# A hybrid decoder block: indexer operands loaded early, query-key passes over 128 rows, softmax divided after the values

## The chip, the cores and the metric

The kernel runs on one core of a Trainium2 chip. The metric is device time in microseconds (us) of one execution. Engines: PE is TensorE (PEld its weight loads), DVE is VectorE, ACT is ScalarE, POOL is GpSimd, SP is SyncE. Each issues its instructions in a fixed order. TensorE's clock has two levels here, 1.2 and 2.4 GHz; the profile gives the granted clock as a share of the higher one.

## The reference, cut to what matters

One layer on 512 tokens of width 1024, in float32. A projection of the normalized input is split into a sparse attention, a recurrence (RWKV-7), a short convolution and three gates; the three results are gated, merged and projected, and a feed-forward part follows. The change concerns the attention:

```python
def one_block(args):                       # 128 queries of each of 4 blocks
    sc = einsum('bqhd,bsd->bqsh', qi_b, ki) * IDX_DIM ** -0.5
    score = einsum('bqsh,bqh->bqs', relu(sc), wi_b)          # the indexer: 8 heads of 64
    score = where(s_idx <= t_b, score, NEG_INF)
    _, sel = top_k(score, n_keep)                            # n_keep = 128
    logits = einsum('bqhd,bqkhd->bqhk', q_b, k[sel]) * ATTN_HEAD_DIM ** -0.5
    bias = rel_bias[t5_bucket(pos_b - positions[sel])]       # a bias by distance
    p = softmax(where(valid, logits + bias, NEG_INF))
    o = einsum('bqhk,bqkhd->bqhd', p, v[sel])                # 8 heads of 64
```

## The kernel before, in words

Matmul operands of 32 bits are split into a high and a low part (`whi`, `wlo`, `h_hi`, `h_lo`); a projection is three passes for each of eight blocks of 128 rows (`mm_t`, L177 to L179, 512 columns; for the value columns `mm_n`, L188 to L190, 256 columns). Weights come by SP's queue into a ring of four raw tiles, ACT makes the high part (L163), POOL the low part (L165, later DVE). A scheduler orders the instructions of each engine when the program is built; the order of the source is the priority. Memory is a stack of pools from the left and one from the right; a tile in reused space waits for the tiles that lay there.

The stages that matter here, in order:

- **Mask stage.** `att_cols` projects indexer queries (slot 2), then `ki` and `wi` (L766, L767), then queries and keys with the steps of `bias_steps` between them: DVE compares positions with thresholds into `mk` tiles (L721, a ring of 18 in the pool `bi`), TensorE sums them into bias tiles, which go to memory as `bias_d`. Queries and keys go to memory as `z_att`, `z_ki`, `z_wi`, each as a high and a low part.
- **Value columns** (L773 to L783), written as `z_v`. Then `bi` closes.
- **Indexer** (L803 to L843). The pools `att` and `ix` open where `bi` was. POOL issues the loads of `qi` (eight) and `ki` (two), SP those of `wiT` and `vtok`. For query blocks 1 to 3 and eight heads, `two_pass` multiplies queries with keys: the first pass takes 128 rows (high and low part of the query, against the high part of the key twice), the second the 64 rows of the high query against the low key. ACT applies relu, DVE sums the heads into `sc` (L832, L834), then finds 128 maxima by sixteen rounds of MAX8 and MATCH_REPLACE8 (L839, L840).
- **Attention** (L855 to L897), four pairs of heads by four query blocks, 16 steps. POOL adds bias and selection (`bt`), `two_pass` (L800, L801) makes the logits, DVE adds `bt` and takes the maximum (L874) and negates it (L876), ACT takes the exponential and its sum (L878), DVE takes the reciprocal and scales the probabilities (L881), TensorE transposes them (L885), ACT copies them to `pT` (L889). After four blocks, 16 matmuls with the values as weights (64 columns of them) and `pT` moving (L894) give the output transposed.
- Beside these stages the gate and branch projections of `branch(1)` and `branch(2)` fill TensorE, and `ada_parts` runs on DVE (L215, L217): it takes blocks of `ada_w` from SP's queue into a ring of three and sums them into `acc`. `branch(0)` needs the attention's output.

`sd_bank` gives one of five PSUM banks, `mm_bank` one of three.

## Time and profile before

| | us |
|---|---|
| median of 3 runs | 1195.21 |
| lowest, highest | 1187.89, 1198.48 |
| the profiled execution | 1197.88 |
| its span, first to last instruction | 1196.2 |
| TensorE busy in it | 1093.3 |
| VectorE busy in it | 763.9 |
| mean granted clock | 0.95 |

A profile row of instructions names the line, the engine, the operation, out<-in, shapes and how many (x); then busy us and mean ns, and after the second bar the engine's idle time just before them with what ended it. A timeline row begins with the start in us and the duration in us; a matmul's duration overlaps the next one's, so the distance of starts is what it costs in a stream.

### The profile page before, as it was taken

The page shows a single profiled execution, that of the slowest core. Times are in us where ns is not written, and L with a number is a line of the kernel's source. Part 1 is how long each engine was busy: PE and PEld are TensorE (multiplying, and loading weights), DVE is VectorE, ACT ScalarE, POOL GpSimd, SP SyncE. Part 2 cuts the span into 40 slices and gives each one's busy share as a digit, 9 for nine tenths or more (in the row PEclk, how much of TensorE's full clock was granted, in tenths as well). Part 3 has the DMA queues.
Part 4 walks back from the last instruction along what each step waited for, and adds up shares of the span by engine and source line. Part 5 has one row for each costly group of instructions (what it writes and reads, how often), then busy time and mean ns, then how long its engine had stood idle before and what let it go on. Part 6 is the DMA issues. An engine that isn't in the chain of part 4 may idle for free.

```text
span 1196.2 us, 17528 instructions
## 1 busy us (share of the span) xinstructions
PE 1093.3 (91%) x6710; PEld 877.2 (73%) x6710; DVE 763.9 (64%) x1363; ACT 447.3 (37%) x765; POOL 363.7 (30%) x254
## 2 busy tenths in 40 slices
PE   4889899799999989998887999998899999999996
PEld 3667678577767875876655778877898888888885
DVE  5888777732587828798555454468866766762326
ACT  4243332132334322422333443446543444542213
POOL 3233233322222430565455210003443455200001
PEclk9899899899989975998899999999999999999998
DMA  9641123322336990279766343522233333462201
GB/s 324 183 107 42 39 75 91 88 61 60 115 98 193 302 247 9 76 208 233 211 186 152 91 132 101 176 84 89 75 85 106 87 90 106 141 229 92 97 5 71
DMA packets 191074, 148.26 MB, mean 124 GB/s; under 512 B 18148, under 2 KB 167038, under 8 KB 190990
## 3 DMA queue, kind: packets, MB, share of 16 engines
q1 hardware_dynamic: 162605, 122.57, 35.5%
q10 hardware_dynamic: 23056, 14.53, 4.1%
q0 software_dynamic: 5328, 10.03, 3.8%
q8 instruction: 53, 0.87, 0.3%
q14 instruction: 32, 0.25, 0.1%
HBM read 128.48 MB, written 18.63 MB: 123 GB/s over the span
## 4 chain that ended last, share of the span: by engine, by line
PE 59%; DVE 21%; issue 8%; DMA 7%; ACT 3%; POOL 2%; SPq 0%; ACTq 0%; DVEq 0%; POOLq 0%
PE mm L177 6%; PE mm L179 6%; PE mm L178 6%; DMA xraw<-in_ada_w 3%; PE sd L177 2%; PE sd L178 2%; PE sd L179 2%; PE sd L801 2%; PE sd L1250 2%; PE sd L1252 2%; PE sd L1251 2%; PE sd L1047 2%; DVE acc L217 2%; PE sd L1049 2%; PE sd L1048 2%
## 5 line engine op out<-in xcount | busy, mean ns | idle before, releaser
L165 POOL TENSOR_TENSOR wlo<-wraw,whi 128x1024 fp32r<-128x1024 f32 (+1 forms) x70 | 157.1, 2246 | 279.6 <-ACT whi L163 222.1
L178 PE MATMUL mm<-h_lo,whi 128*128 128x512 f32 (+2 forms) x496 | 203.3, 410 | 1.5 <-DVE h_lo L1076 1.5
L177 PE MATMUL mm<-h_hi,whi 128*128 128x512 f32 (+2 forms) x496 | 203.7, 412 | 0.7 <-DVE o_cv L702 0.7
L179 PE MATMUL mm<-h_hi,wlo 128*128 128x512 f32 (+2 forms) x496 | 203.4, 410 | 0.0
L163 ACT ACTIVATE whi<-wraw 128x1024 fp32r<-128x1024 f32 (+1 forms) x86 | 80.2, 935 | 221.2 <-PE mm L178 95.2
L178 PEld LDWEIGHTS mm<-h_lo,whi 128*128 128x128 f32 (+1 forms) x496 | 96.2, 194 | 24.5 <-issue 3.3
L177 PEld LDWEIGHTS mm<-h_hi,whi 128*128 128x128 f32 (+1 forms) x496 | 96.0, 194 | 23.0 <-issue 4.2
L179 PEld LDWEIGHTS mm<-h_hi,wlo 128*128 128x128 f32 (+1 forms) x496 | 96.3, 194 | 22.1 <-issue 2.4
L1017 DVE TENSOR_TENSOR wlo<-wraw,whi 128x1024 fp32r<-128x1024 f32 x46 | 64.5, 1403 | 58.9 <-ACT whi L1016 58.3
L1016 ACT ACTIVATE whi<-wraw 128x1024 fp32r<-128x1024 f32 x46 | 48.7, 1059 | 75.7 <-PE sd L1252 27.7
L217 DVE SCALAR_TENSOR_TENSOR acc<-xraw,ccol,acc 128x512 f32<-128x512 f32 x56 | 55.7, 994 | 26.1 <-DMA xraw<-in_ada_w 25.7
L1034 POOL TENSOR_TENSOR fS<-wraw 128x512 f32<-128x512 f32 x13 | 19.8, 1526 | 155.3 <-DMA wraw<-in_ffn_w_up 142.5
L1047 PE MATMUL sd<-mg_hi,shi 128*128 128x256 f32 x156 | 45.1, 289 | 7.8 <-DVE p L1190 7.8
L1017 DVE TENSOR_TENSOR slo<-wraw,shi 128x1024 fp32r<-128x1024 f32 x28 | 34.9, 1247 | 21.6 <-ACT shi L1016 21.5
L721 DVE TENSOR_SCALAR mk<-posq,thr 128x512 f16<-128x512 f32 (+3 forms) x128 | 44.7, 424 | 4.1 <-PE sd L727 4.1
L1293 POOL TENSOR_TENSOR f<-f 128x512 f32<-128x512 f32 x4 | 5.7, 1415 | 134.8 <-ACT wk L993 134.8
L177 PE MATMUL sd<-h_hi,whi 128*128 128x512 f32 x112 | 44.5, 397 | 0.0
L1048 PE MATMUL sd<-mg_lo,shi 128*128 128x256 f32 x156 | 44.4, 285 | 0.0
L1049 PE MATMUL sd<-mg_hi,slo 128*128 128x256 f32 x156 | 44.4, 285 | 0.0
L178 PE MATMUL sd<-h_lo,whi 128*128 128x512 f32 x112 | 44.3, 396 | 0.0
L179 PE MATMUL sd<-h_hi,wlo 128*128 128x512 f32 x112 | 44.2, 395 | 0.0
L177 PE MATMUL mm<-o,whi 128*128 128x512 f32 x96 | 39.9, 416 | 3.2 <-DVE modc L203 3.2
(521 smaller groups left out, 2780.7 us busy)
## 6 DMA issues: line engine op xcount, KB each, us to landing
wraw<-in_w_in SPq DMA_DIRECT2D x61, 512.0 KB, 4.3
xraw<-in_ada_w SPq DMA_DIRECT2D x96, 256.0 KB, 4.4
wraw<-in_ffn_w_up SPq DMA_DIRECT2D x44, 512.0 KB, 3.9
wraw<-in_ffn_w_down SPq DMA_DIRECT2D x22, 512.0 KB, 3.4
wraw<-in_w_branch SPq DMA_DIRECT2D x24, 256.0 KB, 3.8
bias_d<-stage ACTq DMA_DIRECT2D x10, 512.0 KB, 5.2
wraw<-in_w_o SPq DMA_DIRECT2D x8, 512.0 KB, 3.8
z_att<-wk ACTq DMA_DIRECT2D x12, 256.0 KB, 2.2
```

What stands on the lines that cost most here:

```text
L163: ACT.activation(hi, raw, AF.Copy)
L165: lo_engine[0].tensor_tensor(lo, raw, hi, op=ALU.subtract)
L177: PE.matmul(ps, hi[:, k, :], ahi[:, k0 + k, :], start=start and k == 0, stop=False)
L178: PE.matmul(ps, hi[:, k, :], alo[:, k0 + k, :], start=False, stop=False)
L179: PE.matmul(ps, lo[:, k, :], ahi[:, k0 + k, :], start=False, stop=stop and k == kt - 1)
L217: DVE.scalar_tensor_tensor(acc, raw, ck, acc, op0=ALU.mult, op1=ALU.add)
L721: DVE.tensor_scalar(m_[:, :n], posq[:, b * 128:], thr[:, b, gg:gg + 1], None, op0=ALU.is_ge)
L1016: ACT.activation(hi, src, AF.Copy)
L1017: DVE.tensor_tensor(lo, src, hi, op=ALU.subtract)
L1047: PE.matmul(ps, w[0][:, k], b[0][:, k], start=first and k == 0, stop=False, skip_group_check=True)
L1048: PE.matmul(ps, w[0][:, k], b[1][:, k], start=False, stop=False, skip_group_check=True)
L1049: PE.matmul(ps, w[1][:, k], b[0][:, k], start=False, stop=k == 3, skip_group_check=True)
```

## The change

The pools `att` and `ix` open ahead of `bi` and stay beside it; the ring of `mk` has 16 tiles. The loads of `qi`, `ki` and `wiT` are issued by POOL right after `z_ki` and `z_wi` are written, ahead of the query and key projections; `vtok` stays where it was. The second pass of `two_pass` takes 128 rows (both query parts against the low key, twice), in the indexer and in the attention; `kl` is loaded twice for that. In the attention, DVE takes the negated logit and its minimum, each head's exponential follows at once, the transposes take the exponentials undivided, the values are multiplied for each query block with `pT` as weights, and the division is one DVE multiplication of the 128x128 result (`o_tok`), which four transposes then turn.

```diff
+    att = right_pool("att")
+    ix = right_pool("ix")
     bi = right_pool("bi")
...
-                    m_ = T("mk", [128, 512], F16, tag="mk", bufs=18, pool=bi.pool)
+                    m_ = T("mk", [128, 512], F16, tag="mk", bufs=16, pool=bi.pool)
...
     ACT.dma_start(z_wi, t[64:72])
+    vtok = T("vtok", [128, 4, 512], pool=att.pool)
+    sel = {0: cmask}
+    for qb in range(1, 4):
+        sel[qb] = T("sc", [128, (qb + 1) * 128], tag="sc%d" % qb, pool=att.pool)
+    qi = T("qi", [128, 4, 2, 384], F32R, pool=ix.pool)
+    for i in range(4):
+        load_q(qi[:, i], z_att[2, i], 128, 384)
+    ki = T("ki", [128, 2, 512], F32R, pool=ix.pool)
+    for hh in range(2):
+        POOL.dma_start(ki[hh * 64:(hh + 1) * 64], z_ki)
+    wiT = T("wiT", [8, 512], pool=ix.pool)
+    POOL.dma_start(wiT, z_wi)
     att_cols(C_ATT, 0, HD ** -0.5)
     att_cols(C_ATT + MIX, 1, 1.0)
...
     def two_pass(ps, q, hh, q0, k_hi, k_lo, n):
-        r = slice(hh * 64, hh * 64 + 64)
         PE.matmul(ps[:, :n], q[:, hh, q0:q0 + 128], k_hi[:, :n], start=True, stop=False)
-        PE.matmul(ps[:, :n], q[r, hh, q0:q0 + 128], k_lo[r, :n], start=False, stop=True)
+        PE.matmul(ps[:, :n], q[:, hh, q0:q0 + 128], k_lo[:, :n], start=False, stop=True)
...
-        kh, kl = M("kh", [128, 2, 512], F32R), M("kl", [128, 512], F32R)
-        for hh in range(2):
-            POOL.dma_start(kh[hh * 64:(hh + 1) * 64], z_att[1, pr, :, 0, :].rearrange("(h r) t -> r h t", h=2))
-        POOL.dma_start(kl, z_att[1, pr, :, 1, :])
-        pT = M("pT", [128, 4, 640], bufs=1)
+        kh, kl = M("kh", [128, 2, 512], F32R), M("kl", [128, 2, 512], F32R)
+        for i, k in enumerate((kh, kl)):
+            for hh in range(2):
+                POOL.dma_start(k[hh * 64:(hh + 1) * 64], z_att[1, pr, :, i, :].rearrange("(h r) t -> r h t", h=2))
+        o_tok = M("o_tok", [128, 4, 128], bufs=1)
...
-                DVE.tensor_tensor_reduce(lg[hh][:, :n], ps[:, :n], bt[:, hh, :n], 1.0, -3.0e38, op0=ALU.add, op1=ALU.max,
+                DVE.tensor_tensor_reduce(lg[hh][:, :n], ps[:, :n], bt[:, hh, :n], -1.0, 3.0e38, op0=ALU.add, op1=ALU.min,
                                          accum_out=rs[:, 0, hh:hh + 1])
-            DVE.tensor_scalar(rs[:, 1], rs[:, 0], -1.0, None, op0=ALU.mult)
+                ACT.activation(lg[hh][:, :n], lg[hh][:, :n], AF.Exp, bias=rs[:, 0, hh:hh + 1], scale=-1.0,
+                               accum_out=rs[:, 1, hh:hh + 1])
+            DVE.reciprocal(rs[:, 2], rs[:, 1])
+            po = sd_bank()
             for hh in range(2):
-                ACT.activation(lg[hh][:, :n], lg[hh][:, :n], AF.Exp, bias=rs[:, 1, hh:hh + 1], accum_out=rs[:, 2, hh:hh + 1])
-            DVE.reciprocal(rs[:, 0], rs[:, 2])
-            for hh in range(2):
-                DVE.tensor_scalar(lg[hh][:, :n], lg[hh][:, :n], rs[:, 0, hh:hh + 1], None, op0=ALU.mult)
                 pt = sd_bank()
                 for b in range(qb + 1):
-                    j = (b, qb - b)[hh]
-                    PE.transpose(pt[:, j * 128:(j + 1) * 128], lg[hh][:, b * 128:(b + 1) * 128], ident)
...
+                    PE.transpose(pt[:, b * 128:(b + 1) * 128], lg[hh][:, b * 128:(b + 1) * 128], ident)
+                pT = M("pT", [128, 512])
+                ACT.activation(pT[:, :n], pt[:, :n], AF.Copy)
+                h = 2 * pr + hh
+                for b in range(qb + 1):
+                    PE.matmul(po[:, hh * 64:(hh + 1) * 64], pT[:, b * 128:(b + 1) * 128], vtok[:, b, h * 64:(h + 1) * 64],
+                              start=(b == 0), stop=(b == qb))
+            DVE.tensor_tensor(o_tok[:, qb].rearrange("p (h d) -> p h d", h=2), po[:, :128].rearrange("p (h d) -> p h d", h=2),
+                              rs[:, 2].unsqueeze(2).to_broadcast([128, 2, 64]), op=ALU.mult)
         po = sd_bank()
-        for b in range(4):
-            for hh in range(2):
...
+        for qb in range(4):
+            PE.transpose(po[:, qb * 128:(qb + 1) * 128], o_tok[:, qb], ident)
         ACT.activation(o_at[:, pr, :], po, AF.Copy)
```

## Rows read from the trace of the kernel before

**Rows 1.** The page's first part: busy us, share of the span, instructions of each engine.

```profile
PE 1093.3 (91%) x6710; PEld 877.2 (73%) x6710; DVE 763.9 (64%) x1363; ACT 447.3 (37%) x765; POOL 363.7 (30%) x254
```

**Rows 2.** Stretches: length, busy us (instructions) of each engine, granted clock, DMA share, GB/s.

```profile
421.40:438.70 17.30, 12.63 (x85) 12.38 (x84) 0.75 (x1) 4.15 (x5) 5.74 (x4) 0.80 1.12 261
442.00:476.00 34.00, 34.00 (x64) 17.52 (x63) 25.48 (x77) 9.46 (x18) 2.10 (x4) 0.50 0.18 54
476.00:510.00 34.00, 34.00 (x149) 27.01 (x149) 24.90 (x48) 12.71 (x20) 17.92 (x12) 1.00 0.31 86
510.00:557.00 47.00, 43.77 (x190) 35.47 (x189) 46.83 (x76) 13.87 (x22) 30.72 (x20) 0.93 0.75 212
557.00:703.00 146.00, 124.62 (x532) 87.81 (x531) 80.93 (x184) 53.20 (x128) 57.42 (x44) 0.94 0.63 157
703.00:760.00 57.00, 57.00 (x248) 46.16 (x247) 27.08 (x36) 21.23 (x31) 2.95 (x4) 1.00 0.47 130
```

**Rows 3.** TensorE's timeline, last value matmuls and first score passes: start, us, instruction.

```profile
438.36 0.28 PE L188 MATMUL mm<-whi,h_hi 128*128 128x256 f32 x1
438.48 0.28 PE L189 MATMUL mm<-wlo,h_hi 128*128 128x256 f32 x1
...
439.14 0.39 PE L800 MATMUL sd<-ki,qi 128*128 128x256 f32 x1
439.46 0.38 PE L801 MATMUL sd<-ki,qi 64*128 64x256 f32 x1
```

**Rows 4.** TensorE's timeline in the value columns, idle before in brackets.

```profile
424.05 0.38 PE L188 MATMUL mm<-whi,h_hi 128*128 128x256 f32 x1 [2.63 <-ACT whi L163]
426.48 0.58 PE L189 MATMUL mm<-wlo,h_hi 128*128 128x256 f32 x1 [2.04 <-POOL wlo L165]
426.86 0.41 PE L190 MATMUL mm<-whi,h_lo 128*128 128x256 f32 x1
```

**Rows 5.** POOL's timeline: a low part in the mask stage, and the `qi` loads.

```profile
357.56 3.95 POOL L165 TENSOR_TENSOR wlo<-wraw,whi 128x1024 fp32r<-128x1024 f32 x1 [11.84 <-ACT whi L163]
...
414.53 4.82 POOL L796 DMA_DIRECT2D qi<-z_att  x8
```

**Rows 6.** The DMA view of 408 to 440: totals, then an issue with KB each, us.

```profile
DMA packets 8249, 8.52 MB, mean 266 GB/s; under 512 B 522, under 2 KB 6410, under 8 KB 8246
...
qi<-z_att POOLq DMA_DIRECT2D x8, 192.0 KB, 10.2
```

**Rows 7.** The page's costliest groups: the mask comparisons.

```profile
L721 DVE TENSOR_SCALAR mk<-posq,thr 128x512 f16<-128x512 f32 (+3 forms) x128 | 44.7, 424 | 4.1 <-PE sd L727 4.1
```

**Rows 8.** TensorE's timeline in the attention: values, projections, transposes.

```profile
604.77 2.85 PE L894 MATMUL sd<-pT,vtok 128*64 128x512 f32 x16
...
609.15 0.40 PE L178 MATMUL mm<-o,whi 128*128 128x512 f32 x1
609.39 0.40 PE L179 MATMUL mm<-o,wlo 128*128 128x512 f32 x1
...
635.42 1.11 PE L885 MATMUL sd<-ident,lg 128*128 128x128 f32 x8 [2.57 <-DVE lg L881]
```

**Rows 9.** Groups by line, 400 to 710 us: the softmax of the attention.

```profile
L878 ACT ACTIVATE lg<-lg,rs 128x128 f32<-128x128 f32 (+3 forms) x32 | 17.8, 557 | 30.3 <-DVE rs L876 30.3
L881 DVE TENSOR_SCALAR lg<-lg,rs 128x128 f32<-128x128 f32 (+3 forms) x32 | 16.9, 569 | 0.5
L874 DVE CUSTOM_DVE_ANT_0 lg<-sd,bt 128x128 f32<-128x128 f32 (+3 forms) x32 | 15.4, 490 | 25.8 <-PE sd L801 25.3
...
L889 ACT ACTIVATE pT<-sd 128x128 f32<-128x128 f32 (+3 forms) x32 | 12.5, 436 | 32.5 <-PE sd L885 32.5
```

**Rows 10.** Who waited for whom, 408 to 703 us: us in total, times, longest.

```profile
PE sd L885 <- DVE lg L881: 16.7, 10, 3.7
...
DVE acc L217 <- DMA xraw<-in_ada_w: 25.7, 15, 5.1
...
DVE wi L822 <- PE sd L821: 16.1, 1, 16.1
```

**Rows 11.** TensorE's timeline in the recurrence: matmuls of 128x128 weights, 64 columns.

```profile
258.85 1.67 PE L625 MATMUL sd<-UV,HYL 128*128 128x64 f32 x14
```

More of the change, by code (lines that the diff above doesn't have):

```diff
@@ L763, in att_cols, with load_q @@
             split_out(z_att[slot, i], z_col(c0 + i * 128), scale)
+    def load_q(dst, z, t0, n):
+        row = 2 * 512
+        for hh in range(2):
+            src = bass.AP(tensor=z.tensor, offset=z.offset + hh * 512 + t0, ap=[[row, 64], [64 * row + (1 - 2 * hh) * 512, 2], [1, n]])
+            POOL.dma_start(dst[hh * 64:(hh + 1) * 64], src)
     att_cols(C_ATT + 3 * MIX, 2, HD ** -0.5)
@@ L786, in hybrid_block @@
     op_ = left_pool("op")
-    def load_q(dst, z, t0, n):
-        row = 2 * 512
-        for hh in range(2):
-            src = bass.AP(tensor=z.tensor, offset=z.offset + hh * 512 + t0, ap=[[row, 64], [64 * row + (1 - 2 * hh) * 512, 2], [1, n]])
-            POOL.dma_start(dst[hh * 64:(hh + 1) * 64], src)
     def two_pass(ps, q, hh, q0, k_hi, k_lo, n):
-        r = slice(hh * 64, hh * 64 + 64)
         PE.matmul(ps[:, :n], q[:, hh, q0:q0 + 128], k_hi[:, :n], start=True, stop=False)
-        PE.matmul(ps[:, :n], q[r, hh, q0:q0 + 128], k_lo[r, :n], start=False, stop=True)
-    att = right_pool("att")
-    vtok = T("vtok", [128, 4, 512], pool=att.pool)
-    sel = {0: cmask}
-    for qb in range(1, 4):
-        sel[qb] = T("sc", [128, (qb + 1) * 128], tag="sc%d" % qb, pool=att.pool)
-    ix = right_pool("ix")
-    qi = T("qi", [128, 4, 2, 384], F32R, pool=ix.pool)
-    for i in range(4):
-        load_q(qi[:, i], z_att[2, i], 128, 384)
-    ki = T("ki", [128, 2, 512], F32R, pool=ix.pool)
-    for hh in range(2):
-        POOL.dma_start(ki[hh * 64:(hh + 1) * 64], z_ki)
-    wiT = T("wiT", [8, 512], pool=ix.pool)
-    SP.dma_start(wiT, z_wi)
+        PE.matmul(ps[:, :n], q[:, hh, q0:q0 + 128], k_lo[:, :n], start=False, stop=True)
     SP.dma_start(vtok, z_v.rearrange("b p n -> p b n"))
@@ L890, in hybrid_block @@
-        po = sd_bank()
-        for b in range(4):
-            for hh in range(2):
-                h = 2 * pr + hh
-                PE.matmul(po[hh * 64:(hh + 1) * 64, b * 128:], vtok[:, b, h * 64:(h + 1) * 64],
-                          pT[:, b, (b + 1) * 128:] if hh == 0 else pT[:, 3 - b, :(4 - b) * 128],
-                          start=(b == 0), stop=(b == 3), skip_group_check=True)
+                    PE.transpose(pt[:, b * 128:(b + 1) * 128], lg[hh][:, b * 128:(b + 1) * 128], ident)
+                pT = M("pT", [128, 512])
```

8 lines of the change are left out of this document (2 added, 6 removed).

## The prediction

> **What bounds the kernel now.** I read the page's first part, then a table of busy time by stretch, then TensorE's instructions in order of time, then who waits for whom. TensorE is busy 91% of the span, VectorE 64% [rows 1]: TensorE sets the end, and what counts is time in which it stands still, runs at the lower clock or spaces its work out.
>
> The table by stretch shows where that is [rows 2]. In the value columns (421.4 to 438.7) 4.7 us have no matmul, and the granted clock is 0.80. In the indexer's first half (442 to 476) TensorE is "busy" for all 34 us, but at a granted clock of 0.50, the 1.2 GHz level, and with only 64 matmuls. From 510 to 557 it lacks 3.2 us at 0.93; there VectorE is full (46.83 of 47). In the attention (557 to 703) it lacks 21.4 of 146 us at 0.94.
>
> Why 442 to 476 is slow stands in the timeline just before it [rows 3]. Two full-row matmuls of 256 columns start 0.12 us apart (438.36, 438.48), so their weight loads are hidden. The indexer's first passes, also of 256 columns and still at the full clock, start 0.32 us apart (439.14, 439.46): one of 128 rows, one of 64. That alternation is what is new. Under it the clock falls to 1.2 GHz and stays there for 34 us, also for the full-row projections between such pairs.
>
> **The value columns.** TensorE waits 2.63 us for ACT's high part and 2.04 us for POOL's low part of one weight block [rows 4]. Before that POOL spends 4.82 us issuing the eight loads of `qi` [rows 5], in a stretch whose DMA moves 8.52 MB at 266 GB/s with all engines taken; `qi` is 8 x 192 KB of it, 5.8 us at that rate [rows 6], and `ki` comes on top. The change issues these loads right after `z_ki` and `z_wi` are written, into space that no longer waits for the mask tiles. What that can give back here is the standstill, 4.67 us, and the half clock behind it: the 5 us after 426.48, in which a matmul takes 0.41 us [rows 4] instead of 0.28 [rows 3] and starts come at half the rate, some 2.4 us. Bounds 0 and 7. I take 5, because the block for which TensorE stands shares queue and engines with those loads; not all of it, since the `ada_w` loads stay.
>
> What moves in front are eleven POOL issues (eight `qi`, two `ki`, and `wiT`, which leaves SP), at 4.82/8 = 0.60 us each, 6.6 us. POOL has an idle 11.84 us before its low part at 357.56 [rows 5], so I count nothing. Without that cover they push a low part back, and the projection behind it on TensorE: 6.6 us. The mask ring loses two of 18 tiles, so VectorE starts each next half two masks later; TensorE mixes masks with projections there, so I count nothing (worst: 8 halves x 2 masks x 0.42 us [rows 7], 6.8 us).
>
> **128 rows in the indexer.** The 64 matmuls of 442 to 476 would take at most 64 x 0.24 = 15 us at the spacing of full-row matmuls of 512 columns at the full clock (609.15 to 609.39 [rows 8]). That frees 19 us of TensorE. It shortens the kernel as far as VectorE follows, which must finish the top-k before the attention: from 442 to 557 it is busy 25.48 + 24.90 + 46.83 = 97.2 of 115 us [rows 2], so TensorE can bring the end of the top-k forward by 17.8 us at most. I take 14: some of these idle slots come from ACT's hand-over and from projections placed between two score passes, and those remain. Bounds 0 (VectorE waits for something else) and 17.8.
>
> The Trainium skill speaks against this in "TensorE: Matmul & The Clock Gate", Part 3, The mechanism: it says that a weight load overlaps a running matmul only if the two use different row groups. By that, full-row passes would hide no load and the 128 rows would buy nothing, which is the first rival below and its time. The trace does not agree: the full-row matmuls of [rows 3] start 0.12 us apart with a new weight block each.
>
> **128 rows in the attention.** 32 pairs, so 64 passes, each 0.32 - 0.12 = 0.20 us too far apart [rows 3]: 12.8 us. I take 13: the logits on VectorE wait for these passes, so they lie on the chain also where TensorE has slack. Bound below 0, if they fall into its idle time. The second copy of `kl` costs four more POOL issues (2.4 us) and 1 MB, 3.9 us at 266 GB/s; DMA is 0.63 busy over the stage [rows 2], so I count nothing, with 4 us as the bound.
>
> **Softmax divided late.** The 32 scalings of L881 go (mean 569 ns, 16.9 us of VectorE [rows 9]), and 16 small negations. They stood between exponential and transposes, in one in-order queue with the `acc` updates, which wait 25.7 us for `ada_w`; TensorE waited 16.7 us for L881 [rows 10]. Now the transposes wait for ACT alone, and the first head's exponential no longer waits for the second head's logits. Bounds 0 and 16.7; I take 10, because the logits still queue behind `acc`. With fewer standstills about half of the clock loss of this stage (0.06 x 146 = 8.8 us, [rows 2]) should go: 4. The 16 new multiplications read PSUM; nearest is a logit step (490 ns at a mean of 320 columns, [rows 9]), so at most 8 us against 16.9 removed, at the end of a step, where only a bank waits for them. Nothing.
>
> **Probabilities times values.** 64 matmuls in four groups of 16 at 2.85 us [rows 8], 11.4 us, become 80 of 128x128 weights and 64 columns. The nearest row has that shape, in the recurrence: 14 in 1.67 us [rows 11], 0.12 each, so 9.6 us, and 16 transposes at 0.14 (eight in 1.11 us, [rows 8]): 11.8. Equal. But each head's group now follows its ACT copy at once, 32 waits in place of 4, and one step takes two logit banks, one `po` and two transpose banks, all five. A copy takes 436 ns [rows 9]; bounds 0 and 32 x 0.44 = 14 us. I take a loss of 4, because projections can be put between.
>
> **The sum** against the profiled execution (1197.9 us; span 1196.2 and 1.7 around it): 5 + 14 + 13 + 10 + 4 - 4 = 42, so 1155.9. That execution is 2.7 us above the median of the runs, 1195.2; on the median's scale I say 1153. After 703 nothing is touched and TensorE is full (57 of 57 us to 760, [rows 2]), so what is gained ahead stays gained.
>
> **Rivals.** First, 128 rows buy nothing: the load is as exposed as with 64. Then the 14 and the 13 fall away, 5 + 10 + 4 - 4 = 15 remain, less the 4 for `kl`: 1187, within 1%. For it: no row shows these very passes. Against it: the 0.12 us of [rows 3]. Chance 0.08.
>
> Second, VectorE and `ada_w` become the bound. VectorE is full from 510 on [rows 2], and `acc` waits 25.7 us for `ada_w` [rows 10], longer if the same loads are wanted sooner. Then the top-k ends 5 + 8 us earlier, and of the attention's 13 + 10 + 4 - 4 = 23 half is given back: gain 25, 1173. Chance 0.25.
>
> Third, more than forecast: VectorE idles 16.1 us before `wi` [rows 10]. With its operands there much earlier, scores can fill gaps of the mask stage, and the top-k starts while the value columns run. 15 us more: 1141. Against it: projections and masks leave TensorE hardly a gap there. Chance 0.20.
>
> Fourth, slower: with all five banks in one step TensorE, in order, stands through exponential, transposes and copy of each head: 0.557 + 2.5 x 0.14 + 0.436 = 1.34 us [rows 8, 9], 32 times, 43 us, and the 10 and the 4 don't come: 1197.9 - 5 - 14 - 13 + 43 = 1209. It decides from (5 + 14 + 13)/32 = 1.0 us for each head on. Against it: the like waits came to 16.7 us in the old order. Chance 0.07.
>
> **How the numbers follow.** The forecast has 0.40, with its own range 1144 to 1164 (its 14 and its 13 each wrong by a third). With the second and third rival 0.85 of the chance lies between 1138 and 1176; the ends take in the bounds of the terms: all upper ends together, 7 + 17.8 + 13 + 16.7 + 8.8 = 63, give 1132 on the median's scale, and the first rival begins at 1185. So 1132 to 1185. A measurement of this kernel can tell about 1% from no change. Faster by over 1%: 0.40 + 0.25 + 0.20 = 0.85; within 1%: 0.08; slower: 0.07.
>
> **What would show it.** Right: score passes of 256 columns 0.12 us apart, and a granted clock near 1.0 from the first score pass to the end of the indexer; no standstill in the value columns; the top-k over near 538; the attention some 23 us shorter, with less of VectorE in it. Wrong: score passes still 0.3 us apart (first rival); `acc` waiting for `ada_w` well over 25.7 us (second); scores before the value columns (third); TensorE waiting tens of us for the `pT` copy (fourth). And if the clock is low again in the indexer with full rows, it was not the 64 rows that brought it down.

## The result, and the profile after

The changed kernel takes 1179.76 us (median of 4 runs, 1179.11 to 1181.45) where the kernel before takes 1193.03 beside it (4 runs, 1187.89 to 1198.48): ratio 0.989, 95% interval 0.984 to 0.994. A second set of runs gave 0.988 (0.983 to 0.994). A ratio compares only executions within 1.5% of the fastest of their kernel, a median takes all of them, so the two can differ by a few us. The gain is 13 us; 42 were forecast. The direction and the wide range held (1132 to 1185), the size did not.

The page's first part for the changed kernel answers to [rows 1]: TensorE is busy 19.5 us less, VectorE as well. The time in which TensorE isn't busy is 3 us longer (102.9 us of the span before, 105.9 after).

```profile
span 1179.7 us, 17717 instructions
...
PE 1073.8 (91%) x6822; PEld 883.5 (75%) x6822; DVE 744.4 (63%) x1331; ACT 447.9 (38%) x765; POOL 372.3 (32%) x259
```

The table by stretch, as [rows 2], cut where the stages end now: the indexer's score passes, the rest of the indexer, the attention, what follows to the end of the merge, the output projection and what stands beside it, most of the feed-forward part.

```profile
433.70:471.60 37.90, 37.64 (x176) 29.43 (x175) 35.58 (x108) 17.53 (x32) 15.45 (x11) 1.00 0.36 105
471.60:532.70 61.10, 54.60 (x235) 43.95 (x234) 60.74 (x95) 20.60 (x33) 37.09 (x23) 0.92 0.62 177
532.70:650.70 118.00, 98.78 (x521) 79.58 (x521) 51.26 (x138) 47.71 (x116) 59.97 (x49) 0.90 0.84 183
650.70:738.20 87.50, 87.50 (x396) 71.46 (x396) 39.64 (x54) 29.33 (x42) 4.25 (x6) 1.00 0.39 120
738.20:816.30 78.10, 72.44 (x411) 61.94 (x410) 52.80 (x89) 40.82 (x83) 16.37 (x13) 0.98 0.36 111
816.30:1033.60 217.30, 201.73 (x1368) 185.73 (x1367) 150.82 (x184) 97.61 (x149) 90.14 (x61) 0.98 0.34 99
```

The score passes run at the full clock, with VectorE busy 35.58 of 37.90 us. The attention lacks 19.2 of its 118 us at 0.90, a lower clock than the 0.94 of [rows 2]. TensorE's timeline shows the first score passes 0.12 us apart, all of 128 rows, where [rows 3] had 0.32:

```profile
434.44 0.28 PE L813 MATMUL sd<-ki,qi 128*128 128x256 f32 x1
434.56 0.28 PE L812 MATMUL sd<-ki,qi 128*128 128x256 f32 x1
434.67 0.28 PE L813 MATMUL sd<-ki,qi 128*128 128x256 f32 x1
```

Who waited for whom from 471 to 651 us (us in total, times, longest), to set against [rows 10]:

```profile
POOL bt L864 <- DMA bt<-bias_d: 32.7, 6, 11.4
...
DVE acc L217 <- DMA xraw<-in_ada_w: 22.5, 10, 7.4
...
DVE lg L871 <- POOL bt L864: 15.0, 4, 5.9
...
PE sd L880 <- ACT lg L873: 9.9, 6, 3.3
...
PE mm L177 <- DVE modc L203: 6.2, 1, 6.2
...
PE sd L812 <- DMA kh<-z_att: 4.9, 1, 4.9
...
PE sd L891 <- DVE o_tok L887: 3.9, 1, 3.9
```

TensorE's 16.7 us for the scaled probabilities are gone, but the transposes now wait 9.9 us for the exponential, the turned output 3.9 us for a scaling behind `acc`, and projections 6.2 us for the ada columns (3.2 before). The exponential comes from logits that wait in `DVE lg <- POOL bt`, and that in turn for the loads of the bias tiles. GpSimd waited as long for these loads in the kernel before (408 to 703 us, the window of [rows 10]):

```profile
POOL bt L867 <- DMA bt<-bias_d: 34.6, 9, 8.6
```

The group of the new value product, from the groups by line and shape of 433.7 to 738.2, holds the count that the prediction missed:

```profile
L885 PE MATMUL sd<-vtok,pT 128*128 128x64 f32 x160 | 24.7, 287 | 0.5 <-ACT pT L882 0.3
```

### The profile page after: what moved, and what is told of

Same layout as the page of the kernel before. It is cut to its first block, busy times and chain, and to the rows that moved or that the text cites. A ratio compares the mean times of both kernels' runs of the same rounds, so it can differ in the third digit from the quotient of the medians.

```text
span 1179.7 us, 17717 instructions
## 1 busy us (share of the span) xinstructions
PE 1073.8 (91%) x6822; PEld 883.5 (75%) x6822; DVE 744.4 (63%) x1331; ACT 447.9 (38%) x765; POOL 372.3 (32%) x259
## 4 chain that ended last, share of the span: by engine, by line
PE 58%; DVE 19%; issue 8%; DMA 8%; POOL 3%; ACT 2%; SPq 0%; DVEq 0%; POOLq 0%; ACTq 0%
PE mm L177 7%; PE mm L179 7%; PE mm L178 7%; PE sd L177 2%; PE sd L178 2%; PE sd L179 2%; DMA bt<-bias_d 2%; PE sd L1245 2%; PE sd L1246 2%; PE sd L1247 2%; PE sd L1042 2%; DMA wraw<-in_ffn_w_up 2%; PE sd L1044 2%; POOL wlo L165 2%; PE sd L1043 2%
## 5 line engine op out<-in xcount | busy, mean ns | idle before, releaser
L165 POOL TENSOR_TENSOR wlo<-wraw,whi 128x1024 fp32r<-128x1024 f32 (+1 forms) x70 | 162.7, 2327 | 266.4 <-ACT whi L163 216.0
L163 ACT ACTIVATE whi<-wraw 128x1024 fp32r<-128x1024 f32 (+1 forms) x86 | 80.1, 934 | 210.0 <-PE mm L178 99.2
L178 PEld LDWEIGHTS mm<-h_lo,whi 128*128 128x128 f32 (+1 forms) x496 | 96.0, 194 | 21.9 <-DVE h_lo L1071 2.3
L179 PEld LDWEIGHTS mm<-h_hi,wlo 128*128 128x128 f32 (+1 forms) x496 | 96.2, 194 | 19.8 <-issue 0.2
L217 DVE SCALAR_TENSOR_TENSOR acc<-xraw,ccol,acc 128x512 f32<-128x512 f32 x56 | 63.0, 1124 | 29.9 <-DMA xraw<-in_ada_w 29.6
L1012 DVE TENSOR_TENSOR slo<-wraw,shi 128x1024 fp32r<-128x1024 f32 x28 | 34.9, 1246 | 21.5 <-ACT shi L1011 21.4
L1288 POOL TENSOR_TENSOR f<-f 128x512 f32<-128x512 f32 x4 | 5.7, 1414 | 135.0 <-ACT wk L988 135.0
```

The costliest lines, as they stand in the source:

```text
L163: ACT.activation(hi, raw, AF.Copy)
L165: lo_engine[0].tensor_tensor(lo, raw, hi, op=ALU.subtract)
L178: PE.matmul(ps, hi[:, k, :], alo[:, k0 + k, :], start=False, stop=False)
L179: PE.matmul(ps, lo[:, k, :], ahi[:, k0 + k, :], start=False, stop=stop and k == kt - 1)
L217: DVE.scalar_tensor_tensor(acc, raw, ck, acc, op0=ALU.mult, op1=ALU.add)
L1012: DVE.tensor_tensor(lo, src, hi, op=ALU.subtract)
```

## The experiments

Eighteen runs follow, two of them of kernels that had run already. They were made in five groups, each on one chip and beside runs of the kernel before (medians 1188 to 1192). All 86 executions of it in the first four groups have a median of 1189.4. Both profiled executions of it, 1197.9 us, against which the sum was made, and 1197.2, are long ones: stretches compared with them come out some 8 us too favourable together, and no row says which stretch has how much of that. Three stretches are compared, each between landmarks of the timelines: the *indexer*, from the first score pass to the end of the top-k; the *attention*, from there to the last `mg_lo` of the merge, because the scheduler puts other projections beside the attention in each kernel and only at the merge's end has the same work been done; the *feed-forward part*, from its first product to the down projection. Standstill is the attention's length less TensorE's busy time in it.

| kernel | indexer | attention | standstill | feed-forward |
|---|---|---|---|---|
| before, first and second profile | 117.6, 117.6 | 206.9, 207.0 | 21.4, 20.1 | 224.4, 226.2 |
| 128 rows in the indexer alone | 99.3 | 209.6 | 19.8 | 225.6 |
| 128 rows in the attention alone (b_att1) | 117.8 | 196.1 | 26.2 | 224.7 |
| late division alone | 112.8 | 200.1 | 11.5 | 228.2 |
| changed, first and second profile | 98.1, 99.2 | 206.6, 199.3 | 19.2, 16.6 | 230.5, 228.2 |
| changed, other PSUM banks behind the attention (a_rot) | 98.9 | 202.2 | 16.4 | 228.9 |
| changed, old softmax | 98.9 | 198.7 | 25.3 | 223.5 |
| changed, values in fp32r | 98.9 | 199.4 | 20.2 | 226.8 |
| changed, fewer `ada_w` loads | 95.2 | 192.6 | 10.9 | 229.4 |
| changed, no bias tiles | 98.9 | 192.2 | 12.9 | 229.5 |
| changed, neither | 94.9 | 182.8 | 5.2 | 229.2 |

Each kernel but two has one profile. The changed kernel's two and a_rot's have the same list on every engine up to the end of the attention, and show 206.6, 199.3 and 202.2 us for it: a difference of up to 7 us between single profiles can be scatter.

**One part at a time: the indexer's passes.**

```diff
-            two_pass(ps, qi[:, h // 2], h % 2, ...)
+            two_pass_full(ps, qi[:, h // 2], h % 2, ...)     # 128 rows in both passes
```

> The kernel before with one part of the change: the indexer's second pass takes all 128 rows (the keys' low part lies in both halves already). Theory A, TensorE's account: TensorE runs one fixed list of instructions, has nothing in reserve behind the indexer, and so each us of its list that goes is a us of the kernel. The change took the indexer's passes from 24.4 us of TensorE's time to 9.7 and the projections among them 6.4 us shorter by the clock: gain 19 to 23 us, 1170 to 1174, top-k over near 536, granted clock near 1.0 from the first score pass on. Theory B, VectorE and the loads of ada_w bound the attention and give back what is gained ahead of it: gain 8 to 12, 1182 to 1186, with the last attention output no more than 10 us earlier. If the two lengths of the TensorE's row group were not what held the clock down, it stays near 0.5 and the gain is under 5.

Measured: 1180.5 against 1188.1, 7.7 us less by the medians. The ratio, 0.998 (0.994 to 1.001), makes it 3 us, and its interval includes no gain. Stretches of its profile (length, TensorE busy and its instructions, granted clock, DMA share, GB/s):

```profile
439.70:539.00 99.30, 92.28 (x407) 0.97 0.51 151
539.00:748.60 209.60, 189.76 (x804) 0.93 0.57 148
```

and, cut finer, the first half of the indexer, which in [rows 2] had a clock of 0.50:

```profile
439.70:476.00 36.30, 35.79 (x166) 1.00 0.36 109
```

The list of every engine is the same as before, so it was the passes of 64 rows between passes of 128 that held the clock at 1.2 GHz here, and the indexer is 18.3 us shorter. Of these 18 us 11 arrive at the end of this profile (against the second profile of before): 3.3 are lost ahead of the indexer, where nothing was changed, 2.6 in the attention, at a lower clock (0.93, against 0.95 below), and 1.3 behind the merge. In the time of the runs 3 to 8 arrive. Theory A named the stretch; theory B's 8 to 12 is nearer to the time, but that the attention gives the rest back is not shown: 2.6 us are within the scatter of single profiles.

**The attention's passes.** Twice, since the first kernel turned out to change something else:

```diff
-        kh, kl = M("kh", [128, 2, 512], F32R), M("kl", [128, 512], F32R)
+        kh, kl = M("kh", [128, 2, 512], F32R), M("kl", [128, 2, 512], F32R)            # b_att
+        kh, kl = M("kh", [128, 2, 512], F32R), M("kl", [128, 2, 512], F32R, bufs=1)    # b_att1
...
-                two_pass(ps, q, hh, qb * 128, kh[:, hh], kl, max(n, 256))
+                two_pass_full(ps, q, hh, qb * 128, kh[:, hh], kl[:, hh], max(n, 256))
```

> The kernel before with one part of the change: 128 rows in the attention's second pass, with the keys' low part loaded into both halves (8 loads of 256 KB where there were 4). The prediction's term: 13 us, 1181. Theory A, TensorE's account: the passes go from 22.7 us of TensorE's time to 15.4, a gain of 6 to 8, 1186 to 1188. Theory B, VectorE and ada_w bound the stage: no gain, 1192 to 1196, with TensorE's standstills longer by as much as the passes are shorter.

Measured: 1240.9, 53 us slower (1.046, 1.041 to 1.051). In its timeline not one projection matmul stands between the attention's first pass and its last value product; the kernel before has 278 there. The wait view of 508 to 615 us shows TensorE standing in each of the 16 steps:

```profile
PE sd L889 <- DVE lg L885: 51.0, 16, 4.1
```

and it is busy 54.50 of 106.50 us:

```profile
508.50:615.00 106.50, 54.50 (x209) 0.62 0.43 96
```

The Trainium skill, "Perfetto Trace Analysis", section Identifying Performance Opportunities, says that the same gap repeating over a stretch can mean that memory for the next tile is short. This case agrees in part: the next kernel, which gives `kl` one buffer and so needs no more room than before, has 278 projections there again. But the waits in the row above are for the scaled probabilities and not for memory; the second buffer acted on the order of the list, and that it did so by its room is inferred from this pair of kernels.

> The kernel before with 128 rows in the attention, as in b_att, but with one buffer in place of two for the keys' low part, so that the attention's tiles take no more room than before and TensorE's list keeps its 278 projection matmuls between the attention's steps (in b_att there were none). If the loss of 50 us in b_att came from the list, it goes: theory A, the passes 22 to 15 us of TensorE's list: 4 to 8 us faster than before, with the single buffer costing at most 5 us for each of three pairs where the load is late. Theory B: what the passes give is waited for elsewhere, within 3 us of before. If the doubled load itself was the cause, it stays slow, 1230.

Measured: 1176.5 against 1190.7, 14.2 us faster (0.988, 0.983 to 0.994, which is 7 to 20 us): more than theory A's 4 to 8 by the median, and near the prediction's term of 13.

```profile
554.70:750.80 196.10, 169.90 (x793) 0.95 0.67 164
```

The attention is 10.9 us shorter. By the timeline, each record counted from its start to the next start without standstills, the 64 passes take 13.2 us where the second profile of before has 23.8, and the projections 129.6 where it has 135.0; the standstill is 6.1 us longer.

**The late division alone.** The softmax and value product of the change (in the diff ahead) put into the kernel before, with the old passes.

> The kernel before with one part of the change: the softmax divides late, with the new form of probabilities times values (160 matmul records of 64 columns and 16 transposes in place of 64 records), 64 rows in the second passes as before. The prediction's terms: 10 and, of the clock, 4, less 4: gain 10, 1184. Theory A, TensorE's account: probabilities times values take 12.4 us before and 18.8 us after, the transposes of the output 1.5 more, and the standstills do not go but change their cause (16.7 us for the scaled probabilities before; 9.9 for the exponential, 3.9 for the scaled output and 3 more for the ada columns after): a loss of 5 to 9, 1199 to 1203. Between them: the standstills go by half and the two cancel, 1192 to 1196.

Measured: 1191.1 against 1188.1 (1.003, 0.999 to 1.007): no gain. Attention, and feed-forward part:

```profile
552.00:752.10 200.10, 188.58 (x913) 0.97 0.59 155
827.60:1055.80 228.20, 213.17 (x1431) 0.99 0.36 107
```

The standstills do go, 20.1 to 11.5 us, which theory A had denied; the value product takes 18.7 us where it took 12.1, and the attention is 6.9 us shorter than in the second profile of before, which is no more than scatter can be. The time of the runs doesn't show it; 2 to 4 us go in the feed-forward part, which the change doesn't touch. The indexer, 112.8 us, is shorter as well, where only a few instructions of TensorE stand in another place; why is not shown.

**The early loads alone.** The pools, the loads and the mask ring of the change, nothing else.

> The kernel before with one part of the change: the pools of the indexer beside the mask tiles, its loads issued early, 16 mask tiles for 18. The prediction's term: 5 us, 1189, the value columns over 5 us earlier and 1.0 for 0.80 of the clock in them. Theory A: as much, 4 to 6, since TensorE's standstill there is in its one list. The rival: the standstill only moves (the indexer's first passes then wait for something else): no gain, 1192 to 1196, with the end of the top-k where it was.

Measured: 1188.0 against 1188.1 (1.000, 0.996 to 1.005). The 5 us can't be seen in the time. TensorE's standstills in the value columns are 0.69 and 2.04 us, and 0.46 and 1.86 with the other parts, where [rows 4] had 2.63 and 2.04.

**Both kernels again.** Unaltered, for a second profile of each.

> The changed kernel once more, unaltered, with more runs of both kernels and a second profile. In the first two profiles the changed kernel was 24.7 us ahead at the end of the last branch and only 16.5 at the end of the kernel: the feed-forward part, which is the same list of instructions on every engine, took 8 us longer. Theory F1, scatter: that part differs by several us from one execution to the next (432 to 436 in the profiles of five other kernels, 440.8 in this one), so a second profile shows 432 to 437 from the end of the merge. Theory F2, it is caused by the change: 439 to 442 again. Median of the runs 1176 to 1182, against some 1188 for the kernel before: a gain of 6 to 12, not 42.

> The kernel before, unaltered, for a second profile of it. Its first profiled execution (1197.9 us) is among the longer of its runs (1177 to 1211, medians 1188 to 1193). If the execution is an ordinary one the second shows the same stretches: value columns over at 438 to 439, indexer from its first score pass to the end of the top-k 113 to 118 us, from there to the end of the merge 205 to 210, the rest 432 to 434: 1188 to 1198. If the first was an outlier by one stretch, that stretch is 4 us or more shorter here.

Measured: the changed kernel 1175.4 against 1192.3 (0.988); the kernel before 1189.5 against 1188.8 (1.001). Three stretches of the kernel before, second profile:

```profile
436.40:554.00 117.60, 114.37 (x409) 0.83 0.44 127
554.00:761.00 207.00, 186.91 (x803) 0.95 0.58 149
836.60:1062.80 226.20, 213.90 (x1431) 0.98 0.36 108
```

and of the changed one:

```profile
435.50:534.70 99.20, 92.45 (x409) 0.97 0.52 151
534.70:734.00 199.30, 182.69 (x916) 0.96 0.64 160
811.50:1039.70 228.20, 214.92 (x1430) 0.97 0.35 106
```

The two profiles of before agree stage by stage. The two of the changed kernel differ: the first has a longer attention (206.6) and feed-forward part (230.5), with the same lists. The second pair adds up: 0.9 us in the value columns, 18.4 in the indexer, 7.7 in the attention, and 4.0 lost behind the merge make 23.0 us, which is 1195.5 - 1172.5, the difference of the spans. By the medians it is 13 to 17, since the profile of before is a long execution.

**The changed kernel with the old softmax.**

```diff
         # early loads and 128 rows as in the change, kl with one buffer
-        o_tok = M("o_tok", [128, 4, 128], bufs=1)
+        pT = M("pT", [128, 4, 640], bufs=1)
...
+                DVE.tensor_scalar(lg[hh][:, :n], lg[hh][:, :n], rs[:, 0, hh:hh + 1], None, op0=ALU.mult)
```

> The changed kernel with the softmax and the probabilities times values of before (early loads, 128 rows in indexer and attention stay; the keys' second copy has one buffer for two, since two don't fit beside the old pT without TensorE's list losing its projections in the attention). Theory A, TensorE's account: 64 records and 12.4 us for 160 and 18.8, and no transposes of the output; the standstills are about as long either way: faster than the changed kernel by 5 to 8, 1172 to 1175. Theory S, the profile of the kernel before with the new softmax alone (from the end of the top-k to the end of the merge 200.0 us against 207 to 210): slower by 5 to 10, 1185 to 1190.

Measured: 1167.8 where the changed kernel beside it takes 1175.4; against before 0.981 (0.976 to 0.986). As theory A had it, the kernel is faster without the late division: **by 7.6 us** by the medians, with six executions of each (1160 to 1174 against 1170 to 1184), so 8 us give or take 5 by their means.

```profile
531.20:729.90 198.70, 173.41 (x800) 0.95 0.66 161
805.50:1029.00 223.50, 211.77 (x1431) 0.98 0.36 109
```

The attention is as long as the changed kernel's (198.7 and 199.3). By the timeline the late division saves 8.7 us of standstill there and 1.8 in the transposes, and pays 7.6 for the value product (11.1 to 18.7), 2.2 for slower passes (13.1 to 15.3) and 1.4 for turning `o_tok`. So in the attention it brings nothing. The spans differ by 11.1 us all the same: by 3.3 ahead of the indexer, where the lists are the same, by 4.7 in the feed-forward part, which is shorter with the old softmax, and by 1.9 between the merge and that part. Why the kernel with the late division loses time outside that stage is not shown, and the second buffer of `kl`, which only it has, is not told apart.

**Values in half the records.** `vtok` and `pT` in the type fp32r, otherwise the changed kernel.

> The changed kernel with the probabilities and the value rows of the last product in the type that the other matmuls use (fp32r), so that each of the 80 matmuls of 64 columns is one record in place of two; the probabilities and values are rounded by it. The prediction's step reckoned 80 records of 0.12 us; the trace after has 160. Theory A, TensorE's account: some 80 x 0.113 = 9 us of TensorE's list go, 1171 to 1173. If a record of this type with only 64 columns takes twice as long, nothing changes, 1178 to 1182. Theory B, the stage is bound by the bias tiles and ada_w: nothing either, with 9 us more of standstill.

Measured: 1173.9, with 1175.4 for the changed kernel beside it. The value product has 80 records for 160 and 9.0 us for 18.7, as theory A had it, and the attention takes as long as ever (the group of the product, by line and shape, and then the stretch):

```profile
L885 PE MATMUL sd<-vtok,pT 128*128 128x64 f32 x80 | 14.5, 282 | 0.5 <-ACT pT L882 0.3
```

```profile
536.80:736.20 199.40, 179.18 (x834) 0.92 0.64 160
```

The 9.7 us came back as 3.6 us of standstill and, at a clock of 0.92 for 0.96, 6 us in projections, passes and transposes. The time is 1.5 us shorter by the medians, within the spread, so it can't tell theory A from B. The unchanged length of the stage speaks for B, that something other than TensorE's list sets it; but B had 9 us of standstill, and most came back as slower matmuls.

**What sets it: the loads.** First the `ada_w` loads, then the bias tiles, then both.

```diff
             for k in range(8):
+                if k == 0:                                     # a_noada, a_nobtada
-                raw = load_raw([128, 512], [... "ada_w" ...], own=(adp.pool, 3))
+                    raw = load_raw([128, 512], [... "ada_w" ...], own=(adp.pool, 3))
...
-            bt = M("bt", [128, 2, 512])                        # a_nobt, a_nobtada
-            SP.dma_start(bt[:, :, :n], bias_d[...])
-            POOL.tensor_tensor(bt[:, :, :n], bt[:, :, :n], sel[qb]..., op=ALU.add)
...
-                DVE.tensor_tensor_reduce(lg[hh][:, :n], ps[:, :n], bt[:, hh, :n], -1.0, 3.0e38, ...)
+                DVE.tensor_tensor_reduce(lg[hh][:, :n], ps[:, :n], sel[qb][:, :n], -1.0, 3.0e38, ...)
```

> The changed kernel with seven of eight loads of ada_w left out (each ada column uses the first load's values, so the modulation columns are not the reference's); everything else, acc's updates too, stays. From the end of the top-k to the end of the merge the profiles of the changed kernel and of two variants show 199.3, 199.4 and 200.4 us, whether TensorE's list there is 9 us shorter or not: what it loses in records it waits longer. Theory B, the loads of ada_w (and acc, which waits for them, with the softmax queued behind it on VectorE) set that: without them TensorE's standstill there (16 to 19 us) falls to under 8, that stretch to 185 to 190, and the kernel to 1158 to 1165. Theory C, the bias tiles and the order of the steps set it: standstill above 13, 1170 to 1177.

> The changed kernel with the relative bias left out of the logits: no loads of bias tiles and no additions on GpSimd in the attention; the selection mask is added as before. From the end of the top-k to the end of the merge the changed kernel takes 199 to 202 us whatever is taken from TensorE's list, 192.6 without the loads of ada_w. Theory C, the bias tiles (the load, and the addition on GpSimd among the weights' low parts) hold the other half of the standstill: 190 to 194 us here, standstill 16 to 8, the kernel at 1166 to 1170. If they lie beside ada_w and only one of the two ends last at a time, nothing changes: 198 to 202 and 1174 to 1178.

> The changed kernel without the relative bias (as in a_nobt) and with seven of eight loads of ada_w left out (as in a_noada). If the two are the whole floor under the attention, TensorE's standstill from the end of the top-k to the end of the merge falls to under 6 us (only the first loads of keys remain, 3 to 5), that stretch to 183 to 188 and the kernel to 1157 to 1163. If it stays at 190 or more, TensorE waits for the chain of a step itself (passes, logits, exponential, transposes, copy) and not for loads.

Measured: 1166.5, 1163.6 and 1156.6 us, each on its chip, against 1190.7, 1188.8 and 1188.8 for before (0.981, 0.978, 0.973); the changed kernel had 0.988. The first falls between theories B and C, the other two came near the forecast of the theory that blames the loads, a little faster. Beside the first, a_rot, with the changed kernel's lists, takes 1177.7. The attention without `ada_w`:

```profile
534.00:726.60 192.60, 181.72 (x923) 0.96 0.61 138
```

without the bias tiles:

```profile
536.00:728.20 192.20, 179.28 (x914) 0.96 0.57 139
```

and without both:

```profile
537.90:720.70 182.80, 177.56 (x921) 0.99 0.51 117
```

From 199.3 us, the shortest of the three profiles of the changed kernel's list, `ada_w` is worth 6.7, the bias tiles 7.1, both 16.5. Each alone is no more than the scatter between profiles, but the times of the runs fell with them, by some 1% of the kernel each and 1.5% together. Both gone, the stretch is shorter by a little more than the sum of the two, and they take the standstill from 16.6 to 5.2 and the clock to 0.99. So these two streams, with `acc` and `bt` between them and the softmax, hold most of the standstill. Two limits: the bias tiles went with GpSimd's additions, so load and addition are not told apart, and some 199 us are no fixed floor, since 128 rows in the attention alone took 196.1.

**The division on ScalarE.**

```diff
-            DVE.tensor_tensor(o_tok[:, qb]..., po[:, :128]..., rs[:, 2]..., op=ALU.mult)
+                ACT.activation(o_tok[:, qb, hh * 64:(hh + 1) * 64], po[:, hh * 64:(hh + 1) * 64], AF.Copy,
+                               scale=rs[:, 2, hh:hh + 1])
```

> The changed kernel with the late division done by ScalarE (32 copies with a scale, one for each head and step) in place of VectorE (16 multiplications). Theory A: it takes the division out of the queue behind the acc updates, which wait for ada_w: TensorE's 3.9 us for o_tok and POOL's 6.4 us behind it go, 4 to 8 us, 1172 to 1176. Rival: ScalarE's queue is as full of waits (the exponentials wait for the logits), the copies of the probabilities come later behind the divisions, and the time is the same or 2 to 4 us longer, 1179 to 1184.

Measured: 1175.3, the same as the changed kernel beside it. The attention is 200.4 us. The wait for `o_tok` is gone from TensorE, as theory A had it, but the time did not follow: 1175.3 lies in theory A's range only because the changed kernel beside it takes 1175.4. As the rival had it, the time is the same.

**The ada columns in another bank.** The old-softmax kernel with `pm = sd_bank()` for `pm = mm_bank()`.

> The kernel with the early loads, 128 rows in both places and the old softmax (1168 us) with one more edit: the ada columns' last sums take a bank of the five-bank ring in place of the three-bank ring of the projections. TensorE stood 6.18 us before the first projection with o behind one such sum, because VectorE, full of the top-k, had not yet read it. Theory: that standstill goes, 3 to 6 us faster, 1162 to 1165, with TensorE waiting under 1 us for the ada columns. Rival: the projections then run into the next wait (the end of the top-k), since VectorE sets the end of that stage: no change, 1166 to 1170.

Measured: 1165.9 (0.981), as good as without. The wait for the ada columns is gone from its trace, but the scheduler laid out another list (the indexer takes 74 us and the attention 225 in its profile), so the time tells nothing of what that one wait is worth.

**Why the feed-forward part is longer.** The list of every engine in it is the same with both softmaxes, and yet it takes 226.8 to 230.5 us in all nine profiles with the new softmax (mean 228.8), and 222.0 to 226.7 in ten with the old (mean 224.8). About half of the difference is standstill of TensorE, 14.4 us in the mean against 12.1. Three causes were tried: other PSUM banks, and its position in TensorE's and in ScalarE's list.

```diff
+    for _ in range(4):                                         # a_rot: changed kernel, behind the attention
+        sd_bank()
...
+    pad = sd_bank()                                            # o_pad, o_pad2: old softmax
+    for _ in range(58):                                        # at the start; behind the last branch
+        PE.matmul(pad[:, 0:1], ident, one, start=True, stop=True)
...
+    pad = T("sqrt_table", [128, 1])                            # o_pad3: old softmax, behind the last branch
+    for _ in range(25):
+        ACT.activation(pad, merged[:, 7, 0:1], AF.Copy)
```

> The changed kernel with the ring of five PSUM banks turned on by four places after the attention, so that the feed-forward part uses the same banks as in the kernel before; no instruction is added. The feed-forward part (first product to the down projection) took 223.5 to 225.6 us in five profiles with the old softmax and 226.8 to 230.5 in five with the new, with the same list and the same waits on all engines. If it is the banks, this one shows 223 to 226 and the median falls by 4 us, to 1169 to 1173. If not, 227 to 230 and 1174 to 1178.

> The kernel with early loads, 128 rows in both places and the old softmax, with 58 matmuls of one column added at the very start, where TensorE waits for the first loads; nothing reads them. It gives TensorE's list as many instructions ahead of the feed-forward part as the changed kernel has (6802, against 6744). In seven profiles with 6800 to 6804 the feed-forward part took 226.8 to 230.5 us, in seven with 6740 to 6746 223.5 to 226.4, with the same list and waits in it and the same places in memory. If the position in the list does it, 227 to 230 here and a median of 1170 to 1174; if not, 223 to 226 and 1165 to 1169.

> As o_pad, but with the 58 matmuls of one column between the last branch and the output projection, where they can't disturb the start (there they pushed everything back by 19 us). They cost some 58 x 0.1 = 6 us by themselves. If the position in TensorE's list makes the feed-forward part longer, it takes 228 to 230 us (first product to the down projection) and the kernel 1177 to 1180; if not, 223 to 226.5 and 1172 to 1175.

> The kernel with early loads, 128 rows in both places and the old softmax (1168 us), with 25 copies of one column on ScalarE behind the last branch, so that ScalarE's list has as many instructions ahead of the feed-forward part as in the changed kernel (1135 against 1110). In the feed-forward part ScalarE waits 27 to 29.7 us for its weights with the new softmax and 25 to 26 with the old. If the position in ScalarE's list does it, that part takes 228 to 230 us here; if not, 223 to 226.5, and the median is 1168 to 1172.

Measured: with turned banks 228.9 us (median 1177.7, as the changed kernel); with the matmuls at the start 226.7 (1190.7: they pushed everything back by 19 us), which lies between the two cases; behind the branch 225.0 (1192.8); with ScalarE's copies 222.0 (1166.3). By these, with one profile each, none of the three does it. VectorE's list was not tried. The cause of these 4 us stays open.

## Why the prediction was wrong, step by step

**Value columns, 5.** The standstill fell from 4.67 to 2.3 us and the granted clock from 400 to 440 us rose from 0.91 to 1.00 (to 0.95 with the early loads alone); the last value matmul came 4.9 us earlier in the first pair of profiles, 0.9 in the second, and alone it can't be measured in the time. The mechanism held; the size is 0 to 5.

**128 rows in the indexer, 14.** The mechanism held in each point: passes 0.12 us apart, clock 1.00, VectorE full, top-k over at 532.3 and 534.7 (538 was named). The stretch is 18.4 us shorter, a little past the upper bound. The Trainium skill's rule in "TensorE: Matmul & The Clock Gate", Part 3, by which full-row passes would hide no weight load, is not what these traces show (the same section names a background weight buffer as a second way to overlap, and nothing here speaks against that); the first rival fell with it. What is not borne out is the sentence behind it, that what is gained ahead stays gained: alone this part brought 7.7 us by the medians, 3 by the ratio.

**128 rows in the attention, 13.** Near in time: 14.2 us alone, give or take 6. The passes gave 10.6 of the 12.8 that were reckoned; that the projections gave 5.4 more and the standstill took 6.1 was not in the sum. The second copy of `kl`, "counted at nothing" with 4 us as the bound, has a price that no row of time shows, and most likely it is room. Beside the old `pT` it cost the projections between the steps, 53 us slower for 14 faster. The change gets by, it seems, because its `pT` is smaller.

**Softmax divided late, 10 and 4, less 4 for the waits.** The 10 was good by itself: the standstill went by 8.6 us alone and by 8.7 beside the other parts. The 4 for the clock came alone (0.97 for 0.95) but not in the changed kernel (0.94 and 0.96 in its two profiles, 0.96 and 0.95 before). The 4 us lost to `pT` copies hardly came: the matmuls stood 0.3 us for them, though their weight loads waited 6.7 beside matmuls that count as busy.

**Probabilities times values, "Equal".** Here the first step failed: "64 matmuls ... become 80". The 64 of [rows 8] and the 14 of [rows 11] are records of the profile; 80 is the program's count. A matmul of this type leaves two records, so 64 became 160. The product went from 12.1 to 18.7 us alone and from 11.1 to 18.7 in the changed kernel; with the 16 transposes of `o_tok`, a term put at 0.4 us measured 8 and 9. It eats the whole gain in standstill: with and without the late division the attention takes 199.3 and 198.7 us.

**The attention as a whole, 23.** 7.7 by the second pair. By its timelines the passes gave 8.5 us (23.8 to 15.3) where 13 were forecast, the standstill 3.5 where 10 were forecast, projections and transposes 3.8, and the value product with the turning of `o_tok` took 8.0. So the second step that failed is the addition of 13 and 10. With 128 rows alone the standstill rises from 20.1 to 26.2 us, with the late division alone it falls to 11.5, with both it is 16.6: what shorter passes free is in part waited for. Late division alone brings the stretch to 200.1, 128 rows alone to 196.1, both together to 199.3. What TensorE waits for there is in the main the loads of `ada_w` and the bias tiles with their additions: without them the standstill is 5.2 us and the stretch 182.8. That weighs more than the count of records, for with one record per matmul, as reckoned, the stretch was 199.4 in its one profile.

The second rival had this mechanism in part, with half of the 23 given back. It put it down to VectorE and `ada_w`, and `acc` did wait longer, by 4 us (over 408 to 703 us 25.7 before and 29.6 after; 20.4 and 24.7 in the second pair; that window holds more of the attention after than before); the bias tiles, which it didn't name, weigh as much. By gain, 13 to 17 us, the 11 of the first rival are the nearest of the five, ahead of the 25 of the second, and that is luck: the mechanism of the first did not occur. (The prediction states its forecast on the scale of the median, its rivals on that of the profiled execution, 2.7 us higher; so gains are compared here and not times.)

"The attention some 23 us shorter" would have seemed confirmed: from the end of the top-k to the last output it went from 146 to 118 us. But the scheduler had moved 114 of the 278 projection matmuls behind it, where they still had to be done. That sign was badly chosen.

**After 703 us nothing is touched.** So it is, and from the merge on it still took 4 us more in the second pair. That belongs to no term, and its cause stays open.

Together, by medians of one group of runs: early loads and 128 rows, forecast at 32, gave 24.5 with the old softmax; the late division, forecast at 10, took 7.6 away; that leaves 17. So 18 of the 25 us missing there come in with the late division, of which the attention explains that the 10 came to nothing, and not the loss beyond it.

## What to carry to other kernels

When a price comes from a row and a count from the source, put both in one unit first: how many records does one instruction leave? Before two gains in one stage are added, ask what holds the stage when both are there, and take that away in an experiment, here the loads. And an edit that needs a few more kilobytes can change the order of the whole list; look at the order of the list before the time.

## What was not expected of the hardware

The 58 added matmuls of one column kept TensorE "busy" without a gap, 116 records in 21.9 us, and still the granted clock fell to 0.50 under them, the 1.2 GHz level (the timeline's row, and then stretches: length, busy, clock):

```profile
733.27 21.91 PE L958 MATMUL sd<-one,ident 128*128 128x1 f32 x116
```

```profile
725.00:733.00 8.00, 8.00 (x36) 1.00 0.34 121
733.30:740.00 6.70, 6.70 (x47) 0.73 0.53 157
740.00:747.00 7.00, 7.00 (x35) 0.50 0.29 77
747.00:755.00 8.00, 8.00 (x39) 0.50 0.00 0
```

With the alternating rows of [rows 2] that is the second case here of a busy TensorE with a falling clock: a busy TensorE alone doesn't tell the clock, the granted clock's own column does. And in the one profile with half the records in the value product the clock of the attention was 0.92, where three profiles of the changed kernel's list have 0.94, 0.96 and 0.94, and the rest of TensorE's work was slower. That the one caused the other is not shown.
